# Room for 14 overflow blocks in place of 10, a third capacity limit, and a priority mark on the first group's transposes

## The chip, the cores and the metric

The kernel runs on one core of one Trainium2 chip. The core has a matrix engine (TensorE, PE in the profile), VectorE (DVE), ScalarE (ACT), GpSimd (POOL) and SyncE (SP), and 16 DMA engines. The metric is the device time of one execution in microseconds. "Before" is the kernel as it stood, "after" the changed one.

## The reference, cut to what matters

Two trunk layers over 512 latent tokens of width 1024 (layer 0 also carries 256 context tokens as keys and values). Layer 0 mixes tokens by windowed attention, layer 1 by a chunked gMLP. Each mixer is followed by a mixture of experts:

```
for i in range(2):
    hl = modulate(x, sh_a, sc_a)                 # six modulation rows from c @ w_mod[i] + b_mod[i]
    y  = attention(hl, ...) if i == 0 else chunk_gmlp(hl, ...)
    x  = layer_norm(ALPHA * x + g_a * y)
    hl = modulate(x, sh_f, sc_f)
    s  = sigmoid(hl @ router_w)                  # 16 experts, best group of four, two experts per token
    y  = sum over the two experts e of gate_e * ((silu(hl @ w1[e]) * (hl @ w3[e])) @ w2[e])
    x  = layer_norm(ALPHA * x + g_f * y)
```

All weights are fp32. An expert is 1024 x 512 twice and 512 x 1024. How many tokens an expert gets is known only on the chip.

## The kernel before, in words

The program is written in the order of the mathematics, with a tile scheduler that puts the instructions of every engine into a fixed order when the kernel is built. It goes by the order of the text, by which inputs are ready in its own forecast, and by priority: what stands under `tc.high_priority()` is put ahead of what else is ready. At run time each engine runs its own list in that order and waits on semaphores.

**Weights.** All weight pieces (512 KB each) lie in one list, `pieces`, which SP issues in that order, as far ahead as free tiles allow. During attention SP brings the second half of layer 0's modulation weights and the first of layer 1's (`mt`, layer 1, 32 pieces) and then eight pieces of the output projection (`wo`). Between the `mt` pieces stand `zero` pieces: L207 writes zeros to 128 rows of the DRAM buffer `ydr`, each after the last weight load issued (`issue_after`). An `mt` piece is multiplied by a row of the conditioning and summed, either on VectorE (L370) or on GpSimd and ScalarE (L374, L375); after eight pieces the result is turned and written to DRAM (`mdr`, L386 to L389), and read back spread over partitions (L393, L1147).

**Attention.** Scores go to PSUM (L562 to L569), VectorE scales and takes the minimum (L573), ScalarE takes the exponential (L575), PE turns the probabilities (L608), ScalarE copies them out (L609), PE multiplies by the values (L618) and by the reciprocal sums (L628); L632, L634, L635 and L636 make the output tile `OT`, in two halves (high and low part). Then comes the output projection. A `wo` piece is split into a high part on ScalarE (L231, tile `wh`) and a low part on VectorE (L232, tile `wl`); PE multiplies three times per pair (L812, L813, L814) into a PSUM tile `pa`, one for each of the four token tiles, and two such tiles exist. L817 and L818 empty one.

**Mixture of experts.** `plan` counts the tokens of each expert, ranks the experts, and gives the rank its capacity (`VIS`). The units of work (`UNITS`) are 32, 64 or 128 token rows of one expert. Tokens past an expert's capacity go to overflow blocks of 128 rows. `nb` is the number of such blocks for each expert: one if the excess is above 0.5, one more for every limit in L907 that it is above (L908). The total goes to `pint` (L911) and from there to a register on each engine. `more` (L1221) then has the blocks under `tc.If(n > 0)`: lists, block 0, and block i under `tc.If(n > i)` up to NOV. L1281 is the line of that outer If. With a count of zero every engine jumps over all of it. The profiled execution has no row from inside (L1239, L1273) in either layer.

After the block come: L1032 (PE turns the first group's 128 gathered token rows `xg[0]`), L1038 and L1040 (scale and shift into `xt`), the places of the other tokens (`places`, L920 and L922; `tokens`, L1010 and L987), gathers (L1020, L1021), and the units: gemm1 (L1058), silu and product (L1068, L1069), transposes (L1078, L1080), gemm2 (L1091), store (L1097, L1102). SP streams the experts' weights (L226, tile `ring`) all the while. In the end every token gathers its two rows from `ydr` (L1129) and adds them (L1137).

Of the kernel before, what the change touches and what calls it, by code (L numbers as in the profile page):

```python
# [8 lines left out]
F32 = mybir.dt.float32  # L9
# [23 lines left out]

NOV = 10
NR = E - 2


# [67 lines left out]
def hybrid_kernel(ctx: ExitStack, tc: tile.TileContext, A, out):  # L105
# [40 lines left out]
    def small(shape, dt=F32, nm="m", bufs=2):  # L146
        return sm.tile(shape, dt, name=f"{nm}_{nid()}", tag=nm, bufs=bufs)

    def tt2(shape, dt=F32, nm="t"):
        return sm.tile(shape, dt, name=f"{nm}_{nid()}", tag="t2", bufs=9)  # L150
# [3 lines left out]
    pieces = [("mod", 0, j) for j in range(16)]  # L154
# [3 lines left out]
    pieces += [("mt", 0, j) for j in range(16, 48)]  # L158
    for j in range(32):
        pieces += [("mt", 1, j)]  # L160
        if 8 <= j < 8 + 2 * NOV and j % 2:
            pieces += [("zero", (j - 8) // 2)]
    pieces += [("wo", j) for j in range(8)]

    def moe_pieces(l):
# [101 lines left out]
    zero = cst.tile([128, 128], F32, name="zero")  # L267
# [603 lines left out]
    def plan(l):  # L871
# [9 lines left out]
        a = tt2([128, NR, NR], F32, "pa")  # L881
# [22 lines left out]
        V.tensor_tensor(ov, pp, cb[:, 0, :], op=OP.subtract)  # L904
        nb = R["nb"] = small([128, 16], F32, "pnb", 1)
        V.tensor_scalar(nb, ov, 0.5, None, op0=OP.is_gt)
        for lim in (128.5, 256.5):  # L907
            V.scalar_tensor_tensor(nb, ov, lim, nb, op0=OP.is_gt, op1=OP.add)  # L908
        no = small([128, 1], F32, "pno", 1)
        V.tensor_reduce(no, nb, axis=AX.X, op=OP.add)  # L910
# [228 lines left out]
    def moe(l, rest, X):  # L1139
        R = RT[l]  # L1140
        gfr = mdr[l * 4 + 3:l * 4 + 4, :]
        gf = {128: load_row(gfr, alloc=xslot)}
        gs = xslot([128, 768], F32, "gfs")
        gf[64], gf[32] = gs[:, :512], gs[:, 512:]
        for n in (64, 32):
            for h in range(128 // n):
                SC.dma_start(gf[n][h * n:h * n + n, :], gfr[:, h * n * 8:(h + 1) * n * 8].to_broadcast([n, n * 8]))  # L1147
        xg = {}
        slots(l, 0, 1)
        xg[0] = gather(R["gi"][:, 0:1])  # L1150
        with tc.high_priority():
            places, rows, gates = plan(l)
        first = pos["moe", l, 0, 0]
        limit[0] = len(pieces) if l else pos["ws",]
        done = [0]
        units = UNITS[l]
        n = len(units)
        more(l, gf)
        xt = {0: to_xT(l, xg[0])}
        places()  # L1160
        listed = slots(l, 1, 4)
        for g in (1, 2):
            xg[g] = gather(R["gi"][:, g:g + 1])
        pend = None

        def stage(i):
            v = units[i][0]
            lastuse = i + 1 == n or units[i + 1][0] != v

            def adv():  # L1170
                if lastuse:
                    done[0] += 1
                    issue(first + done[0] + LOOK + (0 if l or done[0] < 160 else 4))
            return lambda j: raw("moe", l, v, j), adv

        def fin():
            i, ht = pend
            py = gemm2(units[i][2], ht, *stage(i))
            if i < n - 2:
                store(units[i][2], units[i][3], py, gf)  # L1180
            elif i == n - 2:
                R["py"] = py
            return py

        for i, (v, o, m, row) in enumerate(units):
            g, c = row // 128 - NOV, row % 128
            whole = i + 1 == n or units[i + 1][3] // 128 != row // 128
            p = gemm1(m, xt[g], c, *stage(i))
            s = glu(m, p)
            if i == 0:  # L1190
                with tc.issue_after(rows().ins):
                    rest(0, 4)
            if c == 0 and 2 < g + 2 < NG[l]:
                xg[g + 2] = gather(R["gi"][:, g + 2:g + 3])
            if whole and g + 1 < NG[l]:
                if g:
                    xt[g + 1] = to_xT(l, xg[g + 1])
                else:
                    with tc.issue_after(listed.ins):
                        xt[g + 1] = to_xT(l, xg[g + 1])  # L1200
                if g and g + 3 < NG[l]:
                    slots(l, g + 3, g + 4)
            if i == n // 2:
                gates()
            if i == n - 2 and not l:
                for q in [("winv", j) for j in range(4)]:
                    issue(pos[q] + 1)
                    pairs[q] = split(raws[q])
            if i == n - 4:
                last_slots(l)  # L1210
            if pend:
                fin()
            if i == n - 2:
                collect(l, 1, uslot)
                collect(l, 0, slot)
            pend = (i, to_hT(m, s))
        py = fin()
        limit[0] = len(pieces) if l else pos["moe", 1, 2, 0]
        return py, gf[64]


    def more(l, gf):
        R = RT[l]
        nb, cb = R["nb"], R["cb"]
        n = nc.values_load(R["int"][0:1, NR:], min_val=0, max_val=NOV, skip_runtime_bounds_check_because=why)
        ys = uslot([128, D], F32, "ys")
        xg = uslot([128, D], F32, "xg")
        xt = uslot([128, 8, 128], F32, "xt")
        pre = [slot([128, 1024], F32, "over") for _ in range(3)]
        e16 = cc[:, C_MISC + 8:C_MISC + 8 + NOV]  # L1230
        cum, sh = small([128, 16], F32, "oc", 1), [128, NOV, 16]
        one, eo = small(sh, F32, "oo", 1), small([128, NOV], F32, "oe", 1)
        ko, off = small([128, 4, NOV], F32, "ok", 1), small([128, 16], F32, "of", 1)
        oi, oj = small([128, NOV], I32, "oi", 1), small([128, NOV], I32, "oj", 1)

        def lists():
            buf = tt2([128, 256], F32, "pq").rearrange("p (a b) -> p a b", b=16)
            q = buf
            V.tensor_tensor(q, cc[:, C_T16:C_T16 + 256].rearrange("p (a b) -> p a b", a=16),  # L1239
                            nb[:, None, :].to_broadcast([128, 16, 16]), op=OP.mult)  # L1240
            V.tensor_reduce(cum, q, axis=AX.X, op=OP.add)
            q = buf[:, :NOV, :]
            V.tensor_tensor(q, cum[:, None, :].to_broadcast(sh), e16[:, :, None].to_broadcast(sh), op=OP.is_le)
            V.tensor_reduce(eo, q, axis=AX.X, op=OP.add)
            V.tensor_scalar(eo, eo, 15.0, None, op0=OP.min)
            V.tensor_copy(oi, eo)
            V.tensor_tensor(one, eo[:, :, None].to_broadcast(sh),
                            cc[:, None, C_MISC + 8:C_MISC + 24].to_broadcast(sh), op=OP.is_equal)

            V.tensor_sub(off, cum, nb)  # L1250
            V.scalar_tensor_tensor(off, off, -128.0, cb[:, 0, :], op0=OP.mult, op1=OP.add)
            q = buf[:, :NOV, :]
            V.tensor_tensor(q, one, off[:, None, :].to_broadcast(sh), op=OP.mult)
            V.tensor_reduce(eo, q, axis=AX.X, op=OP.add)
            V.scalar_tensor_tensor(eo, e16, 128.0, eo, op0=OP.mult, op1=OP.add)
            for t in range(4):
                q = buf[:, :NOV, :]
                V.tensor_tensor(q, one, R["key"][:, t, None, :].to_broadcast(sh), op=OP.mult)
                V.tensor_reduce(ko[:, t, :], q, axis=AX.X, op=OP.add)
            V.tensor_tensor(ko, ko, eo[:, None, :].to_broadcast([128, 4, NOV]), op=OP.subtract)  # L1260

            def hot(oh, i, t):
                V.tensor_scalar(oh, iotab, ko[:, t, i:i + 1], None, op0=OP.is_equal)
            tokens(oj, hot, NOV)

        def block(i):
            gather(oj[:, i:i + 1], xg)
            e = nc.values_load(oi[0:1, i:i + 1], engines=[mybir.EngineType.SP], min_val=0, max_val=E - 1,
                               skip_runtime_bounds_check_because=why)
            src = A["moe"][l, bass.ds(e, 1)].rearrange("a j p n -> (a j) p n")  # L1270

            def get(j):
                SP.dma_start(pre[j % 3], src[j])  # L1273
                return pre[j % 3]
            to_xT(l, xg, xt)
            s = glu(128, gemm1(128, xt, 0, get, lambda: None), si)
            py = gemm2(128, to_hT(128, s, hh), get, lambda: None)
            store(128, i * 128, py, gf, ys)

        si, hh = tt2([128, 2, 256], F32, "si"), tt2([128, 512], F32, "hh")  # L1280
        with tc.If(n > 0):  # L1281
            lists()
            block(0)
            for i in range(1, NOV):
                with tc.If(n > i):
                    block(i)
# [133 lines left out]
    p = psA()  # L1420
# [8 lines left out]
    for f in range(8):  # L1429
        wh, wl = hl("winu", f)  # L1430
        p = psB()
# [10 lines left out]
        p = psT()  # L1442
# [110 lines left out]
```

## Time and profile before

| | |
|---|---|
| runs | 1169.61 us median; 1166.64, 1169.61 and 1170.36 |
| profiled execution, its own time | 1169.32 us |
| its span | 1167.5 us |
| mean granted TensorE clock | 0.945 |
| PE busy | 1033.8 us (89%) |
| VectorE, ScalarE, GpSimd busy | 603.8, 348.8, 240.2 us (52%, 30%, 21%) |
| HBM traffic | 310.72 MB read, 21.67 MB written |
| DMA engines' share, queue of the weights (q1) | 64.5% of the span |

The span runs from the first to the last instruction; 1.8 us of the execution's own time lie outside it. The busy shares are means over unlike stages: the profile is read stage by stage, here in windows of the span (attention from about 150 to 283 us, its tail and the projection to 345, the router and plan to 385, layer 0's experts to 640, the gMLP to 845, layer 1's plan to 880, its experts to 1127). A row of the timeline gives the start, the busy time, the engine, line and operation, the tiles, and in brackets for how long the engine had been idle and what released it.

### The profile page before, as it was taken

How to read it: one execution, taken by the hardware profiler on the slowest of the kernel's cores; microseconds unless marked ns; L12 is line 12 of the kernel's file. 1: busy time of each engine (PE TensorE's matmuls, PEld its weight loads, DVE VectorE, ACT ScalarE, POOL GpSimd, SP SyncE). 2: the span in 40 equal slices, each digit the busy share in tenths (PEclk: the TensorE clock that was granted, in tenths of full speed). 3: DMA queues.
4: the chain of work that ended last, by engine and by line, in shares of the span. 5: the costliest groups of instructions: out<-in, count | busy, mean ns of one | idle time of the engine just before them, and what ended most of it. 6: DMA issues, size and time to landing. Idle time of an engine off the chain costs nothing. (4 is left out here: it accounts for less than half of the span.)

```text
span 1167.5 us, 18483 instructions
## 1 busy us (share of the span) xinstructions
PE 1033.8 (89%) x6620; PEld 595.7 (51%) x6620; DVE 603.8 (52%) x1546; ACT 348.8 (30%) x716; POOL 240.2 (21%) x252
## 2 busy tenths in 40 slices
PE   6799799996994899999999679999928999999994
PEld 2577675653783344444443257788824342444531
DVE  1799989876356732222112687886567121211217
ACT  1553397776412111111112234333121110111202
POOL 0044433324000113232022241000011221221140
PEclk9999989998997899999999879999959999999997
DMA  9934447637375899999999602765479999899893
GB/s 352 410 146 166 177 165 243 224 107 252 110 267 213 317 402 345 412 410 410 410 410 366 234 0 109 262 216 171 163 281 357 409 411 410 332 391 407 325 405 132
DMA packets 104283, 330.62 MB, mean 283 GB/s; under 512 B 13345, under 2 KB 24305, under 8 KB 104178
## 3 DMA queue, kind: packets, MB, share of 16 engines
q1 hardware_dynamic: 88608, 287.56, 64.5%
q0 software_dynamic: 10848, 26.75, 6.0%
q10 hardware_dynamic: 4722, 14.98, 3.5%
q8 instruction: 56, 0.92, 0.3%
q14 instruction: 49, 0.40, 0.1%
HBM read 310.72 MB, written 21.67 MB: 285 GB/s over the span
## 5 line engine op out<-in xcount | busy, mean ns | idle before, releaser
L1058 PE MATMUL pb<-ring,xt 128*32 128x256 f32 (+1 forms) x2112 | 225.8, 440 | 0.4 <-DVE ys L1097 0.2
L1058 PEld LDWEIGHTS pb<-ring,xt 128*32 128x32 f32 (+1 forms) x2112 | 87.0, 117 | 112.2 <-issue 71.5
L1102 POOL DMA_DIRECT2D ydr<-ys x132 | 66.7, 511 | 305.0 <-DVE ys L1097 253.0
L1091 PE MATMUL pb<-ring,hh 128*32 128x256 f32 (+1 forms) x1056 | 117.4, 441 | 2.8 <-DMA ring<-in_moe 1.9
L1069 DVE TENSOR_TENSOR si<-si,pb 128x128 f32<-128x128 f32 (+1 forms) x46 | 16.2, 352 | 199.7 <-ACT si L1068 199.7
L370 DVE SCALAR_TENSOR_TENSOR raw<-raw,row 128x1024 f32<-128x1024 f32 x56 | 89.2, 1612 | 0.0
L374 POOL TENSOR_TENSOR raw<-raw,row 128x1024 f32<-128x1024 f32 x24 | 68.1, 2847 | 100.1 <-DMA raw<-in_mt 100.1
L1068 ACT ACTIVATE si<-pb 128x128 f32<-128x128 f32 (+1 forms) x46 | 15.1, 328 | 221.0 <-PE pb L1058 221.0
L1021 POOL DMA_INDIRECT xg<-hdr,Rgi x22 | 24.1, 1096 | 254.3 <-SPq L1281 162.4
L1091 PEld LDWEIGHTS pb<-ring,hh 128*32 128x32 f32 (+1 forms) x1056 | 42.3, 117 | 62.5 <-issue 41.5
L573 DVE TENSOR_SCALAR_CACHE_REDUCE P<-pa,nsink 128x512 f32<-128x512 f32 (+1 forms) x64 | 50.6, 810 | 19.8 <-PE pa L569 11.1
L1058 PE MATMUL pa<-ring,xt 128*128 128x512 f32 x128 | 59.4, 604 | 0.6 <-DVE xt L1040 0.6
L1097 DVE TENSOR_TENSOR ys<-pb,gfs 128x256 f32<-128x256 f32 (+1 forms) x42 | 22.6, 538 | 71.5 <-PE pb L1091 69.4
L1080 ACT COPY hh<-pt 128x128 f32<-128x128 f32 (+2 forms) x50 | 16.9, 338 | 142.4 <-PE pt L1078 135.8
L232 DVE TENSOR_TENSOR wl<-raw,wh 128x1024 fp32r<-128x1024 f32 x44 | 52.5, 1220 | 10.4 <-ACT wh L231 10.2
L575 ACT ACTIVATE P<-P,nm 128x512 f32<-128x512 f32 (+1 forms) x64 | 49.5, 775 | 14.0 <-DVE P L573 13.8
L231 ACT CAST wh<-raw 128x1024 fp32r<-128x1024 f32 x44 | 44.7, 1044 | 10.6 <-DMA mdr<-gr 5.8
L609 ACT COPY PT<-pt 128x512 f32<-128x512 f32 x72 | 39.4, 582 | 27.1 <-PE pt L608 26.9
L608 PE MATMUL pt<-cc,P 128*128 128x128 f32 x288 | 43.8, 281 | 4.1 <-ACT PT L609 3.5
L608 PEld LDWEIGHTS pt<-cc,P 128*128 128x128 f32 x288 | 31.1, 141 | 30.9 <-issue 25.2
L1038 ACT ACTIVATE xt<-pt,bc,gc 128x128 f32<-128x128 f32 x88 | 33.1, 457 | 45.4 <-PE pt L1032 23.0
L1040 DVE TENSOR_SCALAR xt<-pt,gc,bc 128x128 f32<-128x128 f32 x88 | 30.0, 404 | 31.7 <-PE pt L1032 31.7
(376 smaller groups left out, 2020.9 us busy)
## 6 DMA issues: line engine op xcount, KB each, us to landing
ring<-in_moe SPq DMA_DIRECT2D x336, 512.0 KB, 10.5
raw<-in_mt SPq DMA_DIRECT2D x80, 512.0 KB, 5.2
raw<-in_moe SPq DMA_DIRECT2D x48, 512.0 KB, 6.9
raw<-in_mod SPq DMA_DIRECT2D x16, 512.0 KB, 8.4
raw<-in_qkv SPq DMA_DIRECT2D x12, 512.0 KB, 10.2
ydr<-zero SPq DMA_DIRECT2D x10, 512.0 KB, 5.7
ydr<-ys POOLq DMA_DIRECT2D x36, 128.0 KB, 5.7
raw<-in_wo SPq DMA_DIRECT2D x8, 512.0 KB, 5.9
```

The costliest lines, as they stand in the source:

```text
L231: SC.copy(hi, src)
L232: V.tensor_sub(lo, src, hi.bitcast(F32))
L370: m = V.scalar_tensor_tensor(w, w, 1.0, srow[0], op0=OP.mult, op1=OP.mult, accum_out=mv[l][:, j:j + 1])
L374: GP.tensor_mul(w, w, srow[0])
L573: V.tensor_scalar(P[j], reg, -0.125, nsink[:, p * 8 + j:p * 8 + j + 1], op0=OP.mult, op1=OP.min, accum_out=nm[:, j:j + 1])
L575: SC.activation(P[j], P[j], AF.Exp, bias=nm[:, j:j + 1], scale=-1.0, accum_out=sums[:, j:j + 1])
L608: PE.transpose(pt[:, j * 128:(j + 1) * 128], P[a * 4 + j][:, i * 128:(i + 1) * 128], idf)
L609: cp = SC.copy(tl[:, a, :], pt)
L1038: SC.activation(o, i, AF.Identity, bias=b, scale=g)
L1058: PE.matmul(o.rearrange("p (m c) -> p m c", m=2), xt[:, k, c:c + n], w[:, h], start=(k == 0), stop=(k == 7), skip_group_check=True)
L1091: PE.matmul(o, ht[f], w[:, h], start=(f == 0), stop=(f == 3), skip_group_check=True)
L1102: GP.dma_start(ydr[row:row + n, h * n * 8:(h + 1) * n * 8], ys[h * n:h * n + n, :])
```

## The change

Four edits. NOV goes from 10 to 14: four more conditional blocks stand in the program of each layer, `ydr` is longer by 512 rows, the offsets of all units in it move by as much, and there are four more `zero` pieces, which now stand between the `mt` pieces 4 to 31 and not 8 to 27. L907 gets a third limit, 384.5. The call of `to_xT` for the first group, behind the block, stands under `tc.high_priority()`. A tile that is used only inside the block, `one`, comes from another ring.

```diff
-NOV = 10
+NOV = 14
     for j in range(32):
         pieces += [("mt", 1, j)]
-        if 8 <= j < 8 + 2 * NOV and j % 2:
-            pieces += [("zero", (j - 8) // 2)]
+        if 4 <= j < 4 + 2 * NOV and j % 2:
+            pieces += [("zero", (j - 4) // 2)]
     pieces += [("wo", j) for j in range(8)]
...
         V.tensor_scalar(nb, ov, 0.5, None, op0=OP.is_gt)
-        for lim in (128.5, 256.5):
+        for lim in (128.5, 256.5, 384.5):
             V.scalar_tensor_tensor(nb, ov, lim, nb, op0=OP.is_gt, op1=OP.add)
...
         more(l, gf)
-        xt = {0: to_xT(l, xg[0])}
+        with tc.high_priority():
+            xt = {0: to_xT(l, xg[0])}
         places()
...
-        one, eo = small(sh, F32, "oo", 1), small([128, NOV], F32, "oe", 1)
+        eo = small([128, NOV], F32, "oe", 1)
...
             buf = tt2([128, 256], F32, "pq").rearrange("p (a b) -> p a b", b=16)
+            one = tt2([128, 256], F32, "ra").rearrange("p (a b) -> p a b", b=16)[:, :NOV, :]
```

The lines of the changed kernel stand one lower from L1160 on and two lower from L1233 on (L1281 is L1283 there).

PE where layer 1's block ends (its last branch) and the code behind it begins, before: `pt` from `xg` (L1032) are the transposes that the mark is put on.

```order
L1281 UNCONDITIONAL_BRANCH
L987 LDWEIGHTS oh_9407
L987 MATMUL pb_9406<-aux,oh_9407 128x4
...
L987 LDWEIGHTS oh_9439
L987 MATMUL pb_9406<-aux,oh_9439 128x4
L1032 MATMUL pt_9380<-cc,xg_8429 128x128 x4
L1032 MATMUL pt_9389<-cc,xg_8429 128x128 x4
```

The same place after:

```order
L1283 UNCONDITIONAL_BRANCH
L987 LDWEIGHTS oh_10101
L987 MATMUL pb_10100<-aux,oh_10101 128x4
...
L987 LDWEIGHTS oh_10133
L987 MATMUL pb_10100<-aux,oh_10133 128x4
L1032 MATMUL pt_10074<-cc,xg_8778 128x128 x4
L1032 MATMUL pt_10083<-cc,xg_8778 128x128 x4
```

The transposes stand behind the block and behind eight pairs of L987 in both; nothing moved here. In layer 0 they stand directly behind the block's last branch, in both.

PE at the end of attention, before: the last L618 of the values, the two small products L788 and L791, and the projection's third token tile, from the first `wo` piece (`wh590`) on.

```order
1254 L618 MATMUL pb601_2692<-PT613_2740,Vt102_435 64x512 x2
1255 L788 MATMUL pt629_2793<-rwg_628_2791,onesf_104 128x16 x8
1256 L791 MATMUL pt630_2802<-cols_74,bc_627_2787 128x16 x8
1257 L812 MATMUL pa656_2918<-wh590_2668,OT489_2266 128x512
1258 L813 MATMUL pa656_2918<-wl591_2669,OT489_2266 128x512
```

The same place after; `wh634` and `wl635` are the fourth `wo` piece, `pa647` and `pa651` the PSUM tiles of the first two token tiles.

```order
1242 L618 MATMUL pb598_2690<-PT610_2738,Vt102_435 64x512 x2
1243 L788 MATMUL pt626_2791<-rwg_625_2789,onesf_104 128x16 x8
1244 L791 MATMUL pt627_2800<-cols_74,bc_624_2785 128x16 x8
1245 L812 MATMUL pa647_2840<-wh634_2817,OT353_1674 128x512
1246 L812 MATMUL pa651_2880<-wh634_2817,OT443_2070 128x512
1247 L813 MATMUL pa647_2840<-wl635_2818,OT353_1674 128x512
...
1255 L813 MATMUL pa651_2880<-wl635_2818,OT443_2070 128x512
1256 L814 MATMUL pa651_2880<-wh634_2817,OT443_2070 128x512
1257 L812 MATMUL pa655_2920<-wh589_2670,OT489_2268 128x512
```

Twelve matmuls of the first two token tiles, those with the fourth `wo` piece, moved from among the value products to behind them.

VectorE behind the last L634 of attention, before: L634 and L636 make `OT`, L817 empties the first projection tile, L796 and L797 copy the small products.

```order
309 L634 TENSOR_TENSOR rs__617_2760<-pb601_2692,rs__617_2760 128x512
310 L817 TENSOR_TENSOR oz_649_2863<-pa648_2838,row623_2778 128x512
311 L636 TENSOR_TENSOR OT618_2762<-rs__617_2760,OT618_2762 128x512
312 L796 COPY Rse_631_2811<-pt629_2793 128x16
313 L818 SCALAR_TENSOR_TENSOR x619_2770<-x619_2770,oz_649_2863 128x512
314 L232 TENSOR_TENSOR wl638_2820<-raw585_2653,wh637_2819 128x1024
```

And after:

```order
308 L634 TENSOR_TENSOR rs__614_2758<-pb598_2690,rs__614_2758 128x512
309 L636 TENSOR_TENSOR OT615_2760<-rs__614_2758,OT615_2760 128x512
310 L796 COPY Rse_628_2809<-pt626_2791 128x16
311 L232 TENSOR_TENSOR wl635_2818<-raw584_2656,wh634_2817 128x1024
312 L797 COPY Rbe_629_2810<-pt627_2800 128x16
313 L232 TENSOR_TENSOR wl637_2822<-raw585_2658,wh636_2821 128x1024
314 L232 TENSOR_TENSOR wl639_2826<-raw586_2661,wh638_2825 128x1024
315 L817 TENSOR_TENSOR oz_648_2865<-pa647_2840,row620_2776 128x512
```

Three L232 now stand ahead of the first L817, which stood directly behind L634. On ScalarE the fourth L231 (`wh634`) moved from ahead of the last L609 to behind the last L635; `wh636` follows it, then L777, and only then `wh638`, from which `wl639` is made.

## Rows read from the trace of the kernel before

**Rows 1.** Windows by stage: busy us (instructions) per engine, granted clock, DMA share, GB/s.
```profile
205.00:283.00 78.00, 68.91 (x428) 42.50 (x426) 61.90 (x127) 58.39 (x133) 25.67 (x13) 1.00 0.53 182
...
312.00:345.00 33.00, 33.00 (x177) 28.26 (x177) 19.35 (x41) 8.75 (x11) 0.00 (x0) 0.95 0.68 248
...
385.00:640.00 255.00, 252.24 (x2218) 109.05 (x2216) 68.98 (x245) 38.39 (x101) 59.68 (x99) 0.99 1.01 395
```
**Rows 2.** Timeline, layer 0's limits, block count and the jump.
```profile
374.63 0.39 DVE L908 SCALAR_TENSOR_TENSOR pnb<-pov,pnb 128x16 f32<-128x16 f32 x2
...
375.25 0.15 DVE L911 CAST pint<-pno 128x1 int32<-128x1 f32 x1
376.53 1.28 ACT L1038 ACT_TABLE_LOAD   x1 [11.16 <-ACTq L1281]
377.99 0.95 POOL L1020 MEMSET xg<- 128x1024 f32 x1 [3.70 <-remote]
380.62 1.04 DVE L920 TENSOR_TENSOR pq<-Rkey,ppm 128x392 f32<-128x392 f32 x2 [5.22 <-DVEq L1281]
...
380.79 1.94 PE L1032 MATMUL pt<-cc,xg 128*128 128x128 f32 x8 [9.71 <-DVEq L1281]
...
382.77 0.46 ACT L1038 ACTIVATE xt<-pt,bc,gc 128x128 f32<-128x128 f32 x1 [4.95 <-PE pt L1032]
```
**Rows 3.** Timeline, the same place in layer 1.
```profile
872.27 1.04 DVE L920 TENSOR_TENSOR pq<-Rkey,ppm 128x392 f32<-128x392 f32 x2 [4.38 <-DVEq L1281]
872.42 1.32 POOL L1021 DMA_INDIRECT xg<-hdr,Rgi  x1 [162.37 <-SPq L1281]
...
878.15 1.94 PE L1032 MATMUL pt<-cc,xg 128*128 128x128 f32 x8
```
**Rows 4.** DMA view, 872.3 to 873.5 us: that gather, us to landing.
```profile
xg<-hdr,Rgi POOLq DMA_INDIRECT x1, 5.4
```
**Rows 5.** DMA view, 376 to 383 us: packets, MB and share of an instruction queue.
```profile
q14 instruction: 6, 0.05, 2.7%
```
**Rows 6.** Page, DMA issues: the zero pieces, KB each, us to landing.
```profile
ydr<-zero SPq DMA_DIRECT2D x10, 512.0 KB, 5.7
```
**Rows 7.** Timeline of VectorE in attention.
```profile
215.89 1.22 DVE L370 SCALAR_TENSOR_TENSOR raw<-raw,row 128x1024 f32<-128x1024 f32 x1
...
218.28 0.88 DVE L573 TENSOR_SCALAR_CACHE_REDUCE P<-pa,nsink 128x640 f32<-128x640 f32 x1 [1.17 <-PE pt L608]
```
**Rows 8.** Timeline, end of attention and start of the projection.
```profile
289.14 3.89 ACT L231 CAST wh<-raw 128x1024 fp32r<-128x1024 f32 x4 [5.79 <-DMA mdr<-gr]
...
311.44 1.96 PE L788 MATMUL pt<-rwg,onesf 128*128 128x16 f32 x16
311.63 0.69 DVE L634 TENSOR_TENSOR rs__617_2760<-pb,rs__617_2760 128x512 f32<-128x512 f32 x1 [16.78 <-PE pb L618]
...
312.88 1.99 ACT L231 CAST wh<-raw 128x1024 fp32r<-128x1024 f32 x2
...
313.70 0.69 DVE L817 TENSOR_TENSOR oz<-pa,row 128x512 f32<-128x512 f32 x1 [1.38 <-DMA row<-mdr]
...
315.37 0.77 PE L812 MATMUL pa<-wh,OT 128*128 128x512 f32 x1
315.59 1.22 DVE L232 TENSOR_TENSOR wl<-raw,wh 128x1024 fp32r<-128x1024 f32 x1
...
316.53 1.06 ACT L777 ACTIVATE row<-row 128x1024 f32<-128x1024 f32 x1 [1.67 <-DMA row<-in_ln_g]
...
317.65 0.60 PE L814 MATMUL pa<-wh,OT 128*128 128x512 f32 x1
318.07 0.42 PE L812 MATMUL pa<-wh,OT 128*128 128x512 f32 x1
...
318.56 0.40 PE L814 MATMUL pa<-wh,OT 128*128 128x512 f32 x1
318.80 0.39 PE L812 MATMUL pa<-wh,OT 128*128 128x512 f32 x1
```

## The prediction, made before the changed kernel was run

> **What bounds the kernel now.** I read the windows by stage first, then the timeline around each place that the order of instructions shows as changed, and the DMA views last. The windows say which stages pass a delay on [rows 1]. In layer 0's experts PE is busy 252.24 of 255 us and the DMA engines are full as well; layer 1's stage is like it. A later start of such a stage is a later end. The projection behind attention (312 to 345 us) has PE busy for all of its 33 us, so it passes delays on too. Attention (205 to 283 us) is a chain over four engines: PE is busy 68.91 of 78 us, VectorE 61.90, ScalarE 58.39, and the DMA share is only 0.53. There a moved instruction can cost or gain, and an added transfer finds room. The timeline around the conditional block [rows 2, 3] shows that the block is jumped over: between the count (L911) and the rows behind it there are only stretches of idling on the engines' own queues, 5.22 and 4.38 us on VectorE and 9.71 us on PE in layer 0.
>
> **The third limit.** One more L908 per layer, on VectorE, ahead of the reduction, of L911 and so of the branch. Two take 0.39 us [rows 2], so one costs 0.2, and 0.4 over two layers. Everything behind waits for the branch, and both expert stages pass it on. Bounds: 0.3, if part of it lies beside the wait for the branch's fetch, to 0.5.
>
> **The priority mark.** The order of instructions shows L1032 at the same place in both layers: behind the block's last branch in layer 0, behind eight pairs of L987 as well in layer 1. It cannot pass the block, and nothing is gained. Nor was much to be had: in layer 1 the gather that L1032 reads is issued at 872.42 and takes 5.4 us to land [rows 3, 4], that is 877.8 us, and L1032 starts at 878.15. Cost: 0.
>
> **The longer jump.** PE's block grows from 250 to 350 rows, VectorE's from 115 to 151, GpSimd's from 69 to 97, ScalarE's from 51 to 71 and SyncE's from 270 to 378, and none of them runs. The price of the jump in the trace is a wait: in layer 0 VectorE resumes 5.2 us after the count, GpSimd 2.6 (377.99 less the count's end at 375.40), ScalarE 1.1 [rows 2], and in that stretch an instruction queue moves six packets [rows 5]. A jump that already ends in fetched code has no reason to cost more for its length. I take 0 for PE and VectorE, which are on the path. ScalarE has cover: it is needed at 382.77 for L1038, and its table load takes 1.28, so it could resume almost 5 us later in layer 0. GpSimd's rows behind layer 0's branch are for later groups. In layer 1 GpSimd starts the gather at 872.42, the transposes wait for it with 0.35 us to spare, and any delay beyond that counts in full. A second wait like GpSimd's costs 2.6 us a layer; that is the upper bound, 5.2 for both. The lower: if the new position of the code makes the fetch shorter by as much in one layer, -2.6.
>
> The Trainium skill ("Runtime: NRT & Kernel Launch", Instruction fetch mechanics) says that a taken branch whose target is not in the current window of two pages forces a fetch before execution goes on. By that rule a jump that is outside already pays no more for 40% more code, while one that was inside can fall out. The waits and the packets above agree with a fetch; no run here shows how the wait goes with the length. By the rule the sum keeps its 0 for PE and VectorE.
>
> **Four more zero pieces.** 4 x 512 KB on SP's queue, in attention, where DMA has half its time free [rows 1]; a piece lands in 5.7 us [rows 6], and no compute reads it. They begin four `mt` pieces earlier in the list than before and end four later. What hides them is the slack of the `mt` loads. The eight `wo` pieces come right behind. Without that cover the price is one landing, 5.7 us; with it 0. 2 MB at the 395 GB/s of a full stage [rows 1] is 5.3 us of DMA, in a stage with some 36 us free, so I take 0.
>
> **Attention, 205 to 283 us.** The order of VectorE changes where `mt` pieces are multiplied. Before, several L370 stand in a row, PE runs out of scores to turn, and the next L573 idles 1.17 us [rows 7]. After, an L573 stands between the first two of a group. Each such place can give back at most that idling; there are two or three, and the reordering can lose as much elsewhere. Range -2.3 to +2.3; I take half of one idling, -0.6.
>
> **The tail of attention.** This is the largest term. Call T the start of the last L634, 311.63 before [rows 8]. Twelve matmuls with the fourth `wo` piece used to run ahead of T and now stand behind L791. At full clock two follow each other by 0.24 us (318.56, 318.80), so 12 are 2.8 us. T comes earlier by that, less what PE then waits for casts, about 0.8: say T' = T - 2.0. What follows, from T': PE gets to its first L812 at T' + 3.7 (315.37 before). The clock is low there: rows at 317.65 and 318.07 stand 0.42 apart, later ones 0.24. Six of the twelve at 0.42 and six at 0.24 are 4.0, so PE ends them at T' + 7.7. The third token tile needs the first `pa` emptied by L817. On VectorE that now stands behind `wl639`; `wl639` needs `wh638`; and ScalarE makes `wh638` only after L777, which waits for a row from DRAM until T + 4.9 (316.53). From there 1.06 for L777, 1.0 for L231 (1.99 for two), 1.22 for L232 and 0.69 for L817 make T' + 8.9. PE idles 1.2. Lost together: 0.8 + 1.2 = +2.0, in a stage that PE fills. The bounds: -2.0 if T' is early and L817 is not late, since the low clock's stretch is then spent on the twelve as before; +4.0 if T' is no earlier at all.
>
> **Sum.** 0.4 + 0 + 0 + 0 - 0.6 + 2.0 = +1.8 on the profiled execution's 1169.32 (span 1167.5 and 1.8 outside it): 1171.1 us. The median of the three runs is 0.3 above that execution, inside their spread of 3.7, so I add nothing for it.
>
> **Rivals.**
> - *The order is neutral.* The scheduler's moves in attention and its tail cancel, and only L908 is left: 1169.7. For it: PE has work throughout 312 to 345 us, and a stall there may just eat the low clock's stretch. Against it: the chain L777, L231, L232, L817 stands in the order, row by row.
> - *Slower: the jump is fetched twice.* The longer block puts GpSimd or VectorE one more fetch away from the code behind it, in both layers: 2 x 2.6 on the path, with the 0.4 and the tail's half (+1.0) 1175.9. It needs VectorE's idling behind L1281 above 6.5 us in layer 0, or layer 1's gather issued later than 0.35 us past where it is now, measured from L911. For it: the wait was unlike from engine to engine (1.1, 2.6, 5.2), so something in it depends on where the code lies. Against: the longest waits belong to engines that already fetch.
> - *Slower: the zeros delay the loads.* One `wo` piece comes a landing late and half of it shows: 2.9 more than the forecast, 1174.0. Against: DMA is half idle there.
> - *Faster: the gains stay.* Two idlings of L573 go (-2.3) and the tail keeps its -2.0, less 0.4: 1165.4. For it: both are seen in rows. Against: both need every later wait to stand aside.
> - *The mark does nothing,* so the change does not do what it says; that is in the forecast.
>
> **How the numbers follow.** Forecast 0.40, neutral 0.25, longer jump 0.15, late loads 0.07, gains stay 0.13. A measurement of this kernel can tell about 0.3%, 3.5 us, from no change: faster means below 1166.1, slower above 1173.1. Faster: 0.10 of the last case, and 0.03 each of the first two: 0.16. Slower: 0.10 of the forecast (its tail at +4.0 and attention at +2.3 come to 1176.0 at most), 0.01 of neutral, 0.11 of the jump, 0.05 of the loads: 0.27. Same: 0.57. The range runs from 1165.8, about the case of the gains, to 1176.0, the end of the forecast's own bounds and the case of the jump.
>
> **What would show it right or wrong.** In the profile after: three L908 in each layer; no rows from inside the block; L1032 directly behind the same neighbours; VectorE's idling behind the branch at 4 to 6 us. In the tail the first L817 should come 8 us or more behind the last L634, and PE should show an idle of about 1.2 us on `pa`. Windows from 385 on should be as long as before. I am wrong if the expert stages change their length, if the idling at the branch moves by over 1.5 us, or if the tail's L817 comes early.

## The result: 0.7% slower, and the profile after

The changed kernel took 1176.09 us (median of five runs, 1174.62 to 1180.77) against 1167.44 for the kernel before beside it: a ratio of 1.0074 [1.0048, 1.01]. A second set gave 1.0071 [1.0052, 1.009]. That is 8 to 9 us slower. The forecast of 1171.1 had the sign and not the size, and 1176.09 lies just outside the range.

The profiled execution is the slowest of its five runs (span 1179.0 against 1167.5 [rows 1 and the table]), so its stages are read as differences along the way, and the sizes are taken from timed runs. The windows by stage first, shifted to where each stage now lies:

```profile
207.00:285.00 78.00, 66.49 (x416) 40.92 (x414) 59.55 (x126) 57.59 (x129) 32.28 (x15) 1.00 0.55 187
312.00:350.00 38.00, 37.33 (x189) 31.46 (x189) 20.74 (x41) 9.79 (x12) 0.00 (x0) 0.91 0.64 225
390.00:645.00 255.00, 251.99 (x2220) 109.10 (x2218) 68.96 (x245) 38.68 (x102) 59.67 (x99) 0.99 1.00 394
```

Against [rows 1], layer 0's experts are as full as they were. Over the projection's 38 us PE is idle for 0.67 and the mean granted clock is 0.91. The same 38 us before:

```profile
312.00:350.00 38.00, 38.00 (x201) 32.41 (x201) 22.20 (x55) 10.62 (x13) 0.00 (x0) 0.96 0.66 239
```

Now layer 0's branch on the timeline, the answer to [rows 2]:

```profile
379.70 0.59 DVE L908 SCALAR_TENSOR_TENSOR pnb<-pov,pnb 128x16 f32<-128x16 f32 x3
...
380.53 0.15 DVE L911 CAST pint<-pno 128x1 int32<-128x1 f32 x1
381.80 1.28 ACT L1038 ACT_TABLE_LOAD   x1 [11.35 <-ACTq L1283]
383.13 0.95 POOL L1020 MEMSET xg<- 128x1024 f32 x1 [3.77 <-remote]
...
385.52 1.05 DVE L920 TENSOR_TENSOR pq<-Rkey,ppm 128x392 f32<-128x392 f32 x2 [4.84 <-DVEq L1283]
...
385.69 1.94 PE L1032 MATMUL pt<-cc,xg 128*128 128x128 f32 x8 [9.54 <-DVEq L1283]
```

Three L908 take 0.59 us. The jump itself costs VectorE and PE what it did (VectorE idles 4.84 us, before 5.22; PE 9.54, before 9.71), although 40% more code is jumped over. GpSimd comes out 2.45 us behind the count's end, before 2.6. Layer 0's branch lost nothing. In layer 1, the answer to [rows 3]:

```profile
874.59 0.15 DVE L911 CAST pint<-pno 128x1 int32<-128x1 f32 x1
...
878.78 1.04 DVE L920 TENSOR_TENSOR pq<-Rkey,ppm 128x392 f32<-128x392 f32 x2 [4.04 <-DVEq L1283]
...
881.35 2.21 SPq L226 DMA_DIRECT2D ring<-in_moe  x4
...
882.30 1.03 POOL L1021 DMA_INDIRECT xg<-hdr,Rgi  x1 [167.60 <-DVE oh L1010]
...
889.47 1.94 PE L1032 MATMUL pt<-cc,xg 128*128 128x128 f32 x8 [3.30 <-DMA xg<-hdr,Rgi]
```

VectorE is again no later (4.04, before 4.38). GpSimd issues the gather 7.6 us behind the count's end (874.74), before 4.5. By then SP has its weight loads out, and the gather takes 7.0 us to land where it took 5.4 [rows 4]:

```profile
xg<-hdr,Rgi POOLq DMA_INDIRECT x1, 7.0
```

So the transposes start 14.7 us behind the count, 10.3 before, and now it is the gather that ends their wait. What held GpSimd is seen in its queue. The view of the branch's line lists the instructions that are not counted as busy, with the first and the last start (layer 0's and layer 1's). Before, and after:

```profile
L1281 POOLq EVENT_SEMAPHORE  x10: 17/42/43, 376.5 to 869.1; - x10
...
L1281 POOLq COMPARE_BRANCH  x2: 45/45/45, 376.0 to 868.3; - x2
```
```profile
L1283 POOLq EVENT_SEMAPHORE  x10: 17/42/43, 381.8 to 879.0; - x10
...
L1283 POOLq COMPARE_BRANCH  x2: 45/49/53, 381.3 to 875.2; - x2
```

From layer 1's branch to the last semaphore behind it GpSimd took 0.8 us before and takes 3.8 now; in layer 0 the first one comes 0.5 us behind the branch in both. The page's count of packets on one instruction queue grew from 49 to 53:

```profile
q14 instruction: 53, 0.43, 0.1%
```

It is 49 or 50 in every profile of a kernel with 10 blocks, and 53 in every one with 14. So the longer wait goes with more instructions being brought in; that GpSimd waits for them is argued from this, and no row shows it.

### The profile page after: what moved, and what is told of

Its sections match the earlier page's. It is cut to its first block, busy times and chain, and to the rows that moved or that the text cites. A ratio compares the mean times of both kernels' runs of the same rounds, so it can differ in the third digit from the quotient of the medians.

```text
span 1179.0 us, 18492 instructions
## 1 busy us (share of the span) xinstructions
PE 1043.0 (88%) x6620; PEld 601.7 (51%) x6620; DVE 600.2 (51%) x1548; ACT 349.5 (30%) x716; POOL 241.6 (20%) x252
## 5 line engine op out<-in xcount | busy, mean ns | idle before, releaser
L370 DVE SCALAR_TENSOR_TENSOR raw<-raw,row 128x1024 f32<-128x1024 f32 x56 | 85.7, 1545 | 0.0
L1021 POOL DMA_INDIRECT xg<-hdr,Rgi x22 | 23.8, 1083 | 265.7 <-DVE oh L1010 167.6
L573 DVE TENSOR_SCALAR_CACHE_REDUCE P<-pa,nsink 128x512 f32<-128x512 f32 (+1 forms) x64 | 50.7, 810 | 20.5 <-PE pt L608 9.1
L232 DVE TENSOR_TENSOR wl<-raw,wh 128x1024 fp32r<-128x1024 f32 x44 | 52.6, 1218 | 10.2 <-ACT wh L231 9.8
L231 ACT CAST wh<-raw 128x1024 fp32r<-128x1024 f32 x44 | 44.7, 1044 | 9.2 <-DMA mdr<-gr 3.8
L609 ACT COPY PT<-pt 128x512 f32<-128x512 f32 x72 | 39.5, 580 | 23.7 <-PE pt L608 23.5
```

Of the source, the lines that this page charges most:

```text
L231: SC.copy(hi, src)
L232: V.tensor_sub(lo, src, hi.bitcast(F32))
L370: m = V.scalar_tensor_tensor(w, w, 1.0, srow[0], op0=OP.mult, op1=OP.mult, accum_out=mv[l][:, j:j + 1])
L573: V.tensor_scalar(P[j], reg, -0.125, nsink[:, p * 8 + j:p * 8 + j + 1], op0=OP.mult, op1=OP.min, accum_out=nm[:, j:j + 1])
L609: cp = SC.copy(tl[:, a, :], pt)
```

## The experiments

Each ratio is to the kernel before, beside it on the same chip.

**Fewer blocks (b10).** The changed kernel, 10 blocks in the program; every other instruction in the same order.

```diff
-            for i in range(1, NOV):
+            for i in range(1, 10):
                 with tc.If(n > i):
```


> The changed kernel with only 10 conditional blocks in the program (rows for 14 stay, and so do the 14 zero pieces, the third limit and the mark); blocks 10 to 13 are left out of the program, which runs none of them anyway. The order in attention is that of the changed kernel, and layer 1's first gather stands behind the branch as in both. Theory A (the loss has two parts: in layer 1 GpSimd comes out of the longer jump about 3 us later, so that the gather behind it lands 4.5 us later; in the tail of attention the late L817 costs about 3.5): GpSimd's first row behind layer 1's branch returns to 4 to 5 us behind the count, the transposes to 10.3 us behind it, and about half of the loss goes: 1171.3 against 1167.4 before. Theory B (the jump alone): no loss is left, 1167.5 to 1168. Theory C (the moved order in attention alone, the jump's delay is absorbed later): all of the loss stays, 1176.

1175.79 us, 1.0060 [1.0039, 1.0082]. GpSimd's gather went back to 4.5 us behind the count and the transposes to 10.3, as theory A had it, but the time is theory C's: hardly any of it came back.

**The four added zero pieces elsewhere (z14e).** 14 blocks; the tail of attention gets the order of before.

```diff
-        if 4 <= j < 4 + 2 * NOV and j % 2:
-            pieces += [("zero", (j - 4) // 2)]
+        if 8 <= j < 8 + 2 * 10 and j % 2:
+            pieces += [("zero", (j - 8) // 2)]
...
-    pieces += [("mt", 0, j) for j in range(16, 48)]
+    pieces += [q for j in range(16, 48) for q in [("mt", 0, j)] + [("zero", 10 + (j - 18) // 4)] * (j in range(18, 34, 4))]
```


> The changed kernel with the zero pieces elsewhere: ten where they were before, the other four between layer 0's modulation pieces 18 to 30. That gives back the order of before in the tail of attention (48 projection matmuls ahead of the last value product, L817 directly behind L634). 14 blocks stay in the program, and layer 1's first gather stands behind the branch. Theory A: the tail's part goes and the jump's 4.5 us stays: 1172.3, with the transposes of layer 1 at 14 to 15 us behind the count. Theory B: all of the loss stays, 1176. Theory C: none stays, 1167.5 to 1168.

1168.17 us, 0.9993 [0.9974, 1.0013], with the transposes at 15.3 us behind the count. The place of the zero pieces alone takes the changed kernel back to where the kernel before was, though the gather is still late: theory C's number again.

**The same at 33 to 45 (z14f).** As z14e with 33 to 45 in place of 18 to 30.

> As the run with the other four zero pieces between layer 0's modulation pieces, but at 33 to 45. The tail of attention is in the order of before, 14 blocks are in the program, and here the scheduler puts layer 1's first gather ahead of the branch on GpSimd. Theory A: both parts are gone, though the jump is as long as in the changed kernel: 1167.9 (0.4 for the third limit). Theory B with the jump's length itself as the price (VectorE and PE too): 4 us or more stay, 1172 or above. If the four extra zero pieces themselves cost time, it shows here: 1170 or above with no loss at the branch.

1166.19 us, 0.9975 [0.9961, 0.9988]: a little faster than before, with 14 blocks. The gather stands ahead of the branch and the transposes start 5.3 us behind the count, though GpSimd's wait is long here too, 3.4 us from layer 1's branch to the last semaphore:

```profile
L1283 POOLq EVENT_SEMAPHORE  x10: 17/42/43, 377.6 to 869.5; - x10
...
L1283 POOLq COMPARE_BRANCH  x2: 45/45/45, 377.1 to 866.1; - x2
```

What the longer block costs with the gather ahead is not shown: no run has this order with 10 blocks.

**The gather ahead of the branch (ahead).**

```diff
-        more(l, gf)
+        with tc.issue_after(last[0].ins):
+            more(l, gf)
```


> The changed kernel with one edit: the block's branch is put in order behind the first gather, so that in layer 1 the gather's issue stands ahead of the branch on GpSimd (in layer 0 it does already). Order in attention, zero pieces and block length are those of the changed kernel. Theory A: the gather has landed when PE comes out of the jump, the jump's 4.5 us go and the tail's 3.5 stay: 1171.6. Theory B: 1167.5 to 1168. Theory C: 1176, since the wait moves to the next thing behind the branch (the tokens of the other groups).

1171.37 us, 1.0023 [1.0006, 1.0039], theory A's number, and against C: one line at the branch takes back 5 to 6 of the 8 to 9 us. Ahead of the branch nothing else in the order changes, but behind it, from layer 1's experts on, some rows of PE and VectorE move too. The transposes start 8.4 us behind the count, now behind some of the L987 and no longer waiting for the gather:

```profile
876.32 1.03 POOL L1021 DMA_INDIRECT xg<-hdr,Rgi  x1 [158.40 <-DVE peb L892]
877.87 0.15 DVE L911 CAST pint<-pno 128x1 int32<-128x1 f32 x1
...
886.45 1.94 PE L1032 MATMUL pt<-cc,xg 128*128 128x128 f32 x8
```

None of the three theories holds in all four runs. So the jump was measured next with nothing else changed.

**The pairs again (after2, b10_again; z14e_again, z14e_b10).** In both pairs the two kernels differ in the number of blocks alone.

> The changed kernel once more, beside the run with 10 blocks whose order is the same outside the block. Theory A (the longer jump costs 4.4 us in layer 1, the tail about 3): 8 us above the kernel before, 4.4 above the one with 10 blocks; behind layer 1's count GpSimd's gather is issued at 7.6 us and the transposes start at 14.7. Theory D (the later gather moves the stage's start, and the weight stream, which goes on meanwhile, gives most of it back, so that the order in attention is nearly the whole loss): 1 us or less above the one with 10 blocks, at the same late gather.

> The changed kernel with 10 conditional blocks, again (blocks 10 to 13, never run, are left out). Theory A: 4.4 us below the changed kernel measured beside it. Theory D: within 1 us of it.

> The kernel whose tail of attention is in the order of before (four zero pieces between layer 0's modulation pieces), with 10 blocks in the program and not 14; everything outside the block is in the same order as with 14, and layer 1's gather stands behind the branch. Theory A: the gather is issued at 4.5 us behind the count, the transposes start at 10.3, and the time is 4.4 us below the same kernel with 14 blocks: 1164. Theory D: it is within 1 us of it.

> The same with 14 blocks, beside the one with 10. Theory A: 4.4 us above it, gather at 7.7 us and transposes at 15 us behind layer 1's count. Theory D: within 1 us.

| | 14 blocks | 10 blocks |
|---|---|---|
| order of the changed kernel | 1176.98, 1.0071 [1.0052, 1.009] | 1174.16, 1.0048 [1.0032, 1.0065] |
| zero pieces as in z14e | 1167.38, 0.9996 [0.9976, 1.0015] | 1165.55, 0.9971 [0.9955, 0.9986] |

The differences of the ratios are 0.0023 and 0.0025; the changed kernel's first set and b10 gave 0.0014. Each is no larger than its own 95% uncertainty (0.0025 for the two pairs, 0.0034 for the first). Taken together they put the longer jump with the gather behind it at about 2 to 3 us in timed runs (2.6, give or take 1.8), between theory A's 4.4 and theory D's 1, which both lie at the edge of that. Both kernels of the second pair on the timeline, 14 blocks and then 10:

```profile
862.25 0.15 DVE L911 CAST pint<-pno 128x1 int32<-128x1 f32 x1
...
869.93 1.03 POOL L1021 DMA_INDIRECT xg<-hdr,Rgi  x1 [164.05 <-DVE oh L1010]
...
877.90 1.94 PE L1032 MATMUL pt<-cc,xg 128*128 128x128 f32 x8 [4.11 <-DMA xg<-hdr,Rgi]
```
```profile
864.26 0.15 DVE L911 CAST pint<-pno 128x1 int32<-128x1 f32 x1
...
868.95 1.03 POOL L1021 DMA_INDIRECT xg<-hdr,Rgi  x1 [162.76 <-issue]
...
874.50 1.94 PE L1032 MATMUL pt<-cc,xg 128*128 128x128 f32 x8
```

15.5 us against 10.1 behind the count's end: 5.4 us late at the transposes.

**The tail's order alone (late12).** The kernel before, its ten zero pieces four places later.

```diff
-        if 8 <= j < 8 + 2 * NOV and j % 2:
-            pieces += [("zero", (j - 8) // 2)]
+        if 12 <= j < 12 + 2 * NOV and j % 2:
+            pieces += [("zero", (j - 12) // 2)]
```


> The kernel before with one edit: its ten zero pieces stand four modulation pieces later (12 to 31 and not 8 to 27), which ends them where the changed kernel ends its fourteen. Nothing else: 10 blocks, two limits, no mark. The order of VectorE in attention stays that of before word for word, but the tail gets the changed kernel's order (36 projection matmuls ahead of the last value product, L817 behind three L232). Theory E (the end of the zero pieces, and by it the tail's order, is the larger part of the loss): 4 to 6 us above before, 69.5 us from the projection's first matmul to its last against 66 before, and layer 1 as before. Rival F (the moved L573 and L370 in attention, or the four more zero pieces as traffic, make it): no change, 1169.

1168.76 us, 1.0007 [0.999, 1.0024]. A miss for theory E as a price, though its profile has the longer tail. First and last start of L812, before, after, and here:

```profile
L812 PE MATMUL pa<-wh,OT x64: 387/393/797, 290.2 to 356.2; 128*128 128x512 f32 x64
```
```profile
L812 PE MATMUL pa<-wh,OT x64: 387/393/793, 291.8 to 361.3; 128*128 128x512 f32 x64
```
```profile
L812 PE MATMUL pa<-wh,OT x64: 387/393/796, 287.5 to 357.1; 128*128 128x512 f32 x64
```

66.0, 69.5 and 69.6 us. In late12 attention itself, from the first score matmul to the last L573, was 4.7 us shorter than in the two profiles of before (137.8, 142.4 and 142.6): in this one profile it gave in one stage what it took in the next. Its order on VectorE in attention is not quite that of before, though that had been expected: L381, L578 and L634 stand elsewhere in a few places.

**The attention's order alone (early4), and fourteen pieces four places earlier (z14g).** As late12 with 4 in place of 12; the changed kernel with 0 in place of 4.

> The kernel before with its ten zero pieces four modulation pieces earlier (4 to 23). VectorE's order in attention becomes nearly the changed kernel's (an L573 between the L370 of a group), the tail stays as before, 10 blocks. Theory G (attention's order is the rest of the loss): 3 to 5 us above before, 1171 to 1173. Theory H (only where the zero pieces end counts: they take the places of loads that the tail needs): no change or a gain, 1165 to 1169.

> The changed kernel with its fourteen zero pieces four modulation pieces earlier (1 to 27, so that they end where before they did). 14 blocks, three limits, the mark; tail in the order of before; layer 1's first gather behind the long jump. Theory H with the jump's price: 5.6 us above the kernel whose pieces stand at 3 to 29 and whose gather is ahead, so 1168 to 1169; gather at 7.5 us and transposes at 14.5 to 15.5 us behind layer 1's count. Theory G (attention's order): 1171 or above.

early4: 1166.08 us, 0.9979 [0.9959, 0.9998]. The moved L573 and L370 by themselves show no cost, which speaks against theory G. It doesn't leave theory H: late12's pieces end where the changed kernel's do, and it lost nothing. z14g: 1172.9 us, 1.0037 [1.0019, 1.0054], transposes at 16.0 us. That is some 4 us above H's 1168 to 1169, with the tail of before; G's 1171 or above would fit, but failed in early4. Against the kernel before z14g is 4.3 us slower, of which the third limit and the longer jump account for about 3.

**The changed kernel with one number changed (z14h).** Its fourteen zero pieces two places earlier.

```diff
-        if 4 <= j < 4 + 2 * NOV and j % 2:
-            pieces += [("zero", (j - 4) // 2)]
+        if 2 <= j < 2 + 2 * NOV and j % 2:
+            pieces += [("zero", (j - 2) // 2)]
```


> The changed kernel with one number changed: its fourteen zero pieces stand two modulation pieces earlier (3 to 29 and not 5 to 31). 14 blocks, three limits, the mark. The tail gets the order of before, and layer 1's first gather stands ahead of the branch. Theory E with the jump's wait covered by the early gather: at or below before, 1166 to 1169, so 8 us below the changed kernel. Rival F (fourteen zero pieces in this stretch cost by themselves): 1173 or above.

1162.49 us, 0.9947 [0.993, 0.9964]: faster than both kernels and than theory E's 1166 to 1169, with all that the change was to add. The tail is in the order of before (66.2 us from first to last L812), and the scheduler happens to put layer 1's gather ahead of the branch:

```profile
860.21 0.15 DVE L911 CAST pint<-pno 128x1 int32<-128x1 f32 x1
864.40 1.04 DVE L920 TENSOR_TENSOR pq<-Rkey,ppm 128x392 f32<-128x392 f32 x2 [4.04 <-DVEq L1283]
...
865.46 1.94 PE L1032 MATMUL pt<-cc,xg 128*128 128x128 f32 x8 [9.63 <-DVE pq L920]
...
866.70 5.06 SPq L226 DMA_DIRECT2D ring<-in_moe  x5
```

The transposes start 5.1 us behind the count's end, as soon as PE is back.

**The limit and the mark alone (lim_prio), and the kernel before once more (before2).**

> The kernel before with the third limit and the mark alone: 10 blocks, ten zero pieces where they were. The order in attention and its tail is that of before; in layer 1 the scheduler puts the first gather ahead of the branch, as a side effect. Both theories: 0.4 us for two more L908, less up to 2 us for the earlier gather: 1167 to 1169.5.

> The kernel before, unchanged, for a second profile of it: how far its stages move from one profiled execution to the next. Expected: 66 us from the projection's first matmul to its last, 27 us from the experts' last gather product in layer 0 to the gMLP's first, 275 us for layer 1's experts, each within 1.5 us.

lim_prio: 1164.62 us, 0.9974 [0.9959, 0.9989], 3.0 us faster, the 0.4 for two L908 included, a larger gain than was expected (1167 to 1169.5). The gather stands ahead of the branch, and the transposes start 4.6 us behind the count, before 10.3:

```profile
859.96 1.03 POOL L1021 DMA_INDIRECT xg<-hdr,Rgi  x1 [155.33 <-DVE pq L890]
862.23 0.15 DVE L911 CAST pint<-pno 128x1 int32<-128x1 f32 x1
...
867.02 1.30 PE L1032 MATMUL pt<-cc,xg 128*128 128x128 f32 x5 [9.16 <-DVEq L1282]
```

So the new order is worth about 3.4 with the short block. It isn't shown that all of this is the gather's: PE's order moves in layer 0's experts and in the gMLP as well. The built order tells what each line did. The mark alone gives the kernel before word for word on PE, VectorE and ScalarE, the changed kernel without it is the changed kernel, word for word on all five engines, and lim_prio without it is lim_prio. It is the third limit alone that puts the gather ahead here; in the changed kernel, with the same limit, the gather stands behind. before2: one profiled execution, 1172.2 us; 66.2 us from first to last L812, as expected, 28.1 and not 27 to the gMLP's first matmul, 275.9 for layer 1's experts.

## Why the prediction was wrong

**The step that failed.** Two terms of the sum were too small. The one that the runs explain is the longer jump: "I take 0 for PE and VectorE, which are on the path." That holds for them, in both layers. The path in layer 1, though, goes over GpSimd: "GpSimd starts the gather at 872.42, the transposes wait for it with 0.35 us to spare, and any delay beyond that counts in full." The row was read, the condition stated, a price of 2.6 us named, and then nothing of it went into the sum. GpSimd's wait at layer 1's branch rose by 3.0 us, the transposes came 4.4 later, and timed runs put the price at 2 to 3 us. One of the prediction's own signs of being wrong, idling at the branch that moves by over 1.5 us, came true on GpSimd. Where the rest of the 4.4 goes no run shows. That the 2.6 is near these numbers is luck: it was read from layer 0, where GpSimd's first semaphore comes 0.5 us behind the branch and most of the 2.6 is no wait of this kind.

The other term is larger, and its cause stays open. For what the zero pieces do to attention and its tail the sum had -0.6 + 0 + 2.0 = +1.4. With 10 blocks, so without the longer jump, the changed kernel's order is 5.6 to 7.0 us slower than before, 0.4 of it the third limit's. z14e shows that this hangs on the place of the zero pieces; which of the rows that move with it cost the time, no run shows.

The rival "the jump is fetched twice" had the place, at a chance of 0.15, and the second of its signs: layer 1's gather was issued 3.0 us later behind the count. But it took both layers at 2.6 each, and only layer 1's GpSimd fell out. That its 1175.9 is almost the time measured is luck, since the jump gave 2 to 3 us of its 5.2. What the trace before could tell is who had something to lose: an engine that is quick behind the branch, as GpSimd (0.8 us, in both layers) and ScalarE were. That it would be GpSimd, and in layer 1 alone, it couldn't tell. The Trainium skill ("Runtime: NRT & Kernel Launch", Instruction fetch mechanics) says that a taken branch to code outside the window forces a fetch. The trace agrees: VectorE and PE, late before, are no later; GpSimd went from 0.8 to 3.8 us; and four more instruction packets moved, three of them with the four blocks (b10 has 50). No run shows where the window lay, or tells the block's length from the new place of the code behind it.

**The mark** was rightly costed at 0. But the reason that something was to be had from the first group was missed: not the place of L1032 but that of L1021, which in layer 1 stood behind the branch in both kernels. The orders with it ahead are faster by 3.4 us with the short block (lim_prio) and by 5 to 6 with the long one (ahead against the changed kernel); in both some other rows move too.

**The tail** was right in size, +2.0 forecast and 3.0 in profiles (79.5 us from the last L573 to the last L812 after, in both profiles, 76.5 and 76.7 before). Its working holds in some profiles of this order and not in others. VectorE and PE around the last L634, in the first profile after:

```profile
311.46 0.69 DVE L634 TENSOR_TENSOR rs__614_2758<-pb,rs__614_2758 128x512 f32<-128x512 f32 x1 [16.16 <-PE pb L618]
...
318.73 0.69 DVE L817 TENSOR_TENSOR oz<-pa,row 128x512 f32<-128x512 f32 x1 [0.27 <-PE pa L814]
```
```profile
320.20 0.63 PE L814 MATMUL pa<-wh,OT 128*128 128x512 f32 x1
320.63 0.63 PE L812 MATMUL pa<-wh,OT 128*128 128x512 f32 x1
321.05 0.46 PE L813 MATMUL pa<-wl,OT 128*128 128x512 f32 x1
321.35 0.40 PE L814 MATMUL pa<-wh,OT 128*128 128x512 f32 x1
...
327.65 1.07 PE L827 MATMUL pb<-rwg,zt 128*128 128x16 f32 x8 [0.68 <-ACT zt L825]
```

T came 21.4 us behind the first L812 before and 19.7 after, so 1.7 early where 2.0 was said. L777 started 3.7 us behind L634, not 4.9, and L817 ended 8.0 behind it, not 8.9: it waited for the matmuls, and PE had no idle on `pa`. The matmuls behind L791 stood 0.43 apart from 315.36 to 321.05, 5.7 us, at the lower of the clock's two levels, where before it was 2.7 [rows 8] (mean granted clock 0.56 from 315 to 322 us, 0.78 before); the sum had taken half of the twelve at the high clock. In after2, the same program, it went as forecast: 3.1 us at 0.43, L777 5.1 and L817's end 9.0 us behind L634, and PE idle on it:

```profile
317.70 0.50 PE L812 MATMUL pa<-wh,OT 128*128 128x512 f32 x1 [1.08 <-DVE oz L817]
```

ahead and late12 are like it (1.1 and 0.95 us idle); b10 is like the first (5.3 us at 0.43, no idle), b10_again has neither (2.7 us), with a tail of 78.0 us. A long stretch at 0.43 isn't this order's own: z14e and z14f, with the tail of before, have 5.3 and 5.7 us. What all six profiles share, and none with the tail of before, is an idle that the sum lacked: 0.68 us in which PE waits for `zt`, ahead of L827 (PE's last row above). Whether this term stands in the time of the whole is not shown: late12 has the tail and loses nothing.

**Attention and the zero pieces.** -0.6 and 0 in the sum. In early4 the moved L370 shows no cost, and z14h, with four more pieces in the same stretch, is the fastest of all, so as traffic they show none either. L908 is 0.2 a piece, as said.

**What stays open.** 0.4 and 2 to 3 are about 3 of the 8 to 9 us. With 10 blocks the changed order still stands 5.6 to 7.0 above before, and it is neither the tail alone (late12) nor attention alone (early4, whose attention is nearly in that order). In all five profiles with that order the gMLP's first matmul (L443) comes 28.2 to 29.1 us behind layer 0's first L703 (a product at the end of its experts), in the other profiles 25.9 to 28.1, and layer 1's count 194.3 to 195.2 us behind that matmul, in the others 190.0 to 194.1. With the tail's 3.0 that is most of it, but one profile moves by 1 to 3 us in each stage. No run tells why. All that is shown is that the place of the zero pieces, which changes the built order in many places, decides: with 10 blocks it makes the kernel 3.4 us faster than before (z14e_b10) or 5.6 to 7.0 slower (b10).

## What to carry to other kernels

A jump over code that doesn't run is not free for what stands behind it: see for each engine how long it takes from the branch to its first instruction, find the ones that are quick, and ask what they would hold up if they became slow like the others. Put the issue of a gather ahead of the branch. Raising the priority of its consumer moved nothing here, with the gather behind the branch or ahead of it, and the built order shows that before anything is timed.

When an edit changes the place of a few transfers in a list, build the neighbours too: two places decided between 0.7% slower and 0.5% faster here, and the diff shows nothing of it.

## What was not expected of the hardware

- GpSimd's wait at layer 1's branch, to the last semaphore behind it, had three sizes: 0.8 us with 10 blocks, 3.4 to 3.9 in most kernels with 14, and 1.6 in two of those with the gather ahead (ahead, z14h). VectorE came out 3.9 to 4.7 us behind layer 1's count in all of them.
- The gather of 128 rows took 5.4 us to land when it was issued ahead of the weight loads and 7.0 behind them (before, after).
- The transposes started 4.2 to 5.4 us later for the longer block, and about half of it was in the timed runs.
